# Two of eight depthwise convolutions computed by even and odd tokens on the matrix engine, and three smaller moves in a two-layer encoder trunk

## Chip, cores and metric

One core of a Trainium2 chip. The metric is the device time of one execution in microseconds (us). Its engines are named as in the profile: PE (TensorE, matrix products), PEld (its weight loads), DVE (VectorE), ACT (ScalarE), POOL (GpSimd) and SP (SyncE, which here issues nearly all DMAs).

## What is computed

A trunk of two layers on 512 tokens x 1024 features, float32. Each of four sub-layers is modulated by a vector c and closed by a gated residual and a LayerNorm:

```
def _modulation(c, w, b):
    m = jax.nn.silu(c) @ w + b
    shift, scale, gate = jnp.split(m, 3, axis=-1)
...
x <- LayerNorm(alpha*x + (1+gate) * f(x*(1+scale)+shift))
```

Layer 0 is a mixer (a spatial-gating MLP and a multi-scale pooling side by side), then a gated FFN with a depthwise convolution of width 3. Layer 1 is a conformer convolution, then a second FFN. The conformer convolution is

```
def _conformer_conv(h, w_in, dw, dw_b, ln_g, ln_b, w_out):
    a, g = jnp.split(h @ w_in, 2, axis=-1)
    z = a * jax.nn.sigmoid(g)
    z = _depthwise_conv(z, dw, dw_b)          # width 31, 1024 channels
    z = jax.nn.silu(_layer_norm(z, ln_g, ln_b))
    return z @ w_out
```

## The kernel before, in words

**Products.** Every large product runs on PE in three parts (`mm3`, L179): both operands are split into a high part that the fast fp32r format holds and a low remainder, and hi x hi, hi x lo and lo x hi are added in PSUM. `parts` (L150) splits a weight tile of 128x1024: ACT or DVE casts `whi`, DVE subtracts to `wlo`; both names have rings of 7 buffers. Activations are `hhi`/`hlo` or `ahi`/`alo` in the same way. A 512-column product has 512 columns of one operand streamed past 128x128 of the other.

**Opening (L124 to L520).** c is fetched into all 128 partitions (`cb`, 512 KB), ACT takes silu of it, and 24 PE transposes of a piece of `cb` against the identity (`WAKE`) follow. The modulation needs silu(c) @ w; DVE takes it as dots of rows of `in_ada` with `cb` (`ada_dot`, two per k, into the tiles `x`, which serve as staging). `project(k)` (L489) then scales the k-th block of x with them (ACT), splits it (`hhi`, `hlo`) and issues 24 products, 8 outputs of 3 parts each, output by output. k runs from 0 to 7. For k = 0 DVE makes both `whi` and `wlo`.

**FFN of layer 0 (about 145 to 511 us).** 22 pairs of 128 channels. Beside its PE work, `side0`/`ahead0` prepare layer 1: dots of the remaining modulations, split matrices of `cv_in` and `cv_out`, and 128x128 diagonal matrices, one per tap, that hold a tile's 128 tap weights (`diagonal`, L755, POOL, 2 x 62 steps). Split or built pairs are written to DRAM (`keep`) and later fetched into the `whi`/`wlo` rings (`recall`).

**Conv stage (about 511 to 700 us).** `to_next` (L397) closes the FFN: for each of four row tiles s of 128 tokens, DVE adds the residual, takes statistics, centres and scales `x`, PE transposes it, ACT modulates, DVE subtracts `hlo`. It then starts the first four column tiles of the next projection. The eight channel tiles follow: `proj_tiles` (two tiles `pa`, `pg`), `glu` (z = pa * sigmoid(pg), DVE), then the convolution of width 31 of that tile. The table `CONV` (L27) shares a tile's 31 taps out, for both halves of the tokens together or one by one: (number of taps on PE, number on POOL with ACT), the rest on DVE. A DVE tap is one SCALAR_TENSOR_TENSOR of 512 or 256 columns, a POOL tap an ACT scaling and a POOL addition, a PE tap three products of 256 columns with a diagonal matrix. Before, tile 6 has all 31 taps on PE in both halves, tile 7 has 31 on PE in the first half, tile 3 is wholly on DVE.

The two halves of the tokens (`hf`) are finished one after the other. `by_rows` (L936) transposes the convolved tiles `cvs` so that tokens are rows, and DVE takes statistics; the tiles come in the order of `CONV_END` (0, 2, 1, 3, 6, 4, 5, 7), two per call. `normalise` (L950) follows, `back` (L967) transposes again, applies gain, bias and silu (ACT) and splits, and `out` (L1017) adds the output product with the kept `cv_out` pairs. `advance(later[2], T_FILL)` places PE taps of the second half between `normalise` and `back`.

**The residual's affine step.** `finish_x` (L298) multiplies one half (d) of the columns of one row tile of x with the LayerNorm's gain row and adds its bias row: two steps. For the LayerNorm that stands before the conv stage these are 8 + 8 steps at the end of the stage: most of the first 8 on POOL, the last 8 on DVE (`finish(8, V, ...)`, L1042); the rows are fetched by `ln_rows` on ACT's queue at L986.

**Order.** Each engine runs its instructions in a fixed order. A scheduler writes it from the program order and its own estimates; `pin`, `behind` and the two flags `in_order`, `pool_order` hold pieces of it in the order of the program.

## Time and profile before

| what | value |
|---|---|
| median of 3 runs | 1071.51 us (1069.69 to 1071.95) |
| the profiled execution's own time | 1072.34 us |
| its span in the profile | 1070.6 us |
| mean granted clock of PE | 0.994 of full |
| DMA | 214.23 MB, mean 200 GB/s |

The span is the time from the first to the last instruction of the profiled execution; its own time has what lies around it too. Times in the rows below are us from the start of the span. A row of a timeline may stand for several equal instructions (x4), and its duration is then that of all. PE's products are pipelined: the distance from one start to the next is what a product costs, and the duration shown is longer. The profile puts nearly every instruction at L85, the helper that records them, so instructions are told apart by the names of their tiles.

### The profile page before, as it was taken

The page shows a single profiled execution, that of the slowest core. Times are in us where ns is not written, and L with a number is a line of the kernel's source. Part 1 is how long each engine was busy: PE and PEld are TensorE (multiplying, and loading weights), DVE is VectorE, ACT ScalarE, POOL GpSimd, SP SyncE. Part 2 cuts the span into 40 slices and gives each one's busy share as a digit, 9 for nine tenths or more (in the row PEclk, how much of TensorE's full clock was granted, in tenths as well). Part 3 has the DMA queues.
Part 4 walks back from the last instruction along what each step waited for, and adds up shares of the span by engine and source line. Part 5 has one row for each costly group of instructions (what it writes and reads, how often), then busy time and mean ns, then how long its engine had stood idle before and what let it go on. Part 6 is the DMA issues. An engine that isn't in the chain of part 4 may idle for free.

```text
span 1070.6 us, 13947 instructions
## 1 busy us (share of the span) xinstructions
PE 1046.3 (98%) x5157; PEld 883.5 (83%) x5157; DVE 787.3 (74%) x1173; ACT 461.4 (43%) x676; POOL 269.7 (25%) x309
## 2 busy tenths in 40 slices
PE   7999999999999999999999999899999999999997
PEld 5888798888888888888988987798888888888886
DVE  6789879989866889966399999767675333666537
ACT  4544374333743444533666743474444212444400
POOL 0000200068026950002199995200000022000011
PEclk9999999999999999999999999999999999999999
DMA  9969508777999998981555480233433233232302
GB/s 356 406 231 378 199 27 272 268 255 265 371 416 365 327 337 312 333 313 59 221 213 191 158 276 36 99 103 124 126 100 99 99 99 99 97 94 91 103 9 79
DMA packets 61555, 214.23 MB, mean 200 GB/s; under 512 B 6960, under 2 KB 6960, under 8 KB 61488
## 3 DMA queue, kind: packets, MB, share of 16 engines
q1 hardware_dynamic: 59184, 209.16, 54.7%
q10 hardware_dynamic: 2304, 4.20, 1.4%
q8 instruction: 40, 0.66, 0.2%
q14 instruction: 27, 0.22, 0.1%
HBM read 182.13 MB, written 31.20 MB: 199 GB/s over the span
## 4 chain that ended last, share of the span: by engine, by line
PE 87%; DVE 5%; DMA 3%; POOL 3%; issue 1%; ACT 0%; SPq 0%; DVEq 0%; POOLq 0%
PE ps L85 87%; POOL whi L85 1%; DVE a L85 1%; POOL wlo L85 1%; DMA w<-in_ffn_up 1%; DVE x L85 1%; DMA w<-in_ab_in 1%; DVE wlo L85 1%; DVE t L85 1%; DVE st L85 1%; DMA w<-in_cv_out 1%; DVE ps L85 1%; DMA whi<-keephi_cv_out 0%; ACT whi L85 0%; POOL x L85 0%
## 5 line engine op out<-in xcount | busy, mean ns | idle before, releaser
L85 PE MATMUL ps<-hhi,whi 128*128 128x512 f32 (+1 forms) x960 | 353.1, 369 | 0.0
L85 PE MATMUL ps<-hhi,wlo 128*128 128x512 f32 (+1 forms) x960 | 353.0, 368 | 0.1
L85 PE MATMUL ps<-hlo,whi 128*128 128x512 f32 (+1 forms) x960 | 353.0, 368 | 0.0
L85 DVE TENSOR_TENSOR wlo<-w,whi 128x1024 fp32r<-128x1024 f32 x176 | 218.3, 1246 | 164.8 <-ACT whi L85 160.9
L85 ACT CAST whi<-w 128x1024 fp32r<-128x1024 f32 x175 | 182.6, 1049 | 303.4 <-PE ps L85 185.7
L85 PEld LDWEIGHTS ps<-hhi,wlo 128*128 128x128 f32 x960 | 181.0, 189 | 30.5 <-DVE wlo L85 0.5
L85 PEld LDWEIGHTS ps<-hlo,whi 128*128 128x128 f32 x960 | 181.1, 189 | 29.8
L85 PEld LDWEIGHTS ps<-hhi,whi 128*128 128x128 f32 x960 | 180.7, 189 | 29.7
L85 POOL TENSOR_TENSOR x<-x,t 128x512 f32<-128x512 f32 x32 | 48.4, 1540 | 531.4 <-DVE t L85 531.4
L85 PE MATMUL ps<-whi,ahi 128*128 128x512 f32 (+1 forms) x426 | 165.4, 388 | 0.0
L85 PE MATMUL ps<-wlo,ahi 128*128 128x512 f32 (+1 forms) x426 | 164.3, 386 | 0.0
L85 PE MATMUL ps<-whi,alo 128*128 128x512 f32 (+1 forms) x426 | 164.2, 385 | 0.0
L85 DVE SCALAR_TENSOR_TENSOR t<-ps,cols,t 128x511 f32<-128x511 f32 x176 | 130.0, 744 | 5.9 <-ACT t L85 4.4
L85 POOL TENSOR_TENSOR a<-a 128x512 f32<-128x512 f32 (+1 forms) x99 | 104.5, 1092 | 22.9 <-ACT a L85 22.5
L85 ACT ACTIVATE t<-ps,cols 128x512 f32<-128x512 f32 (+1 forms) x108 | 78.0, 738 | 41.4 <-PE ps L85 39.7
L85 PEld LDWEIGHTS ps<-whi,ahi 128*128 128x128 f32 x426 | 80.1, 188 | 17.0 <-issue 0.5
L85 PEld LDWEIGHTS ps<-wlo,ahi 128*128 128x128 f32 x426 | 80.1, 188 | 16.4 <-issue 0.5
L85 PEld LDWEIGHTS ps<-whi,alo 128*128 128x128 f32 x426 | 80.1, 188 | 16.0
L85 ACT ACTIVATE a<-a,cols 128x512 f32<-128x512 f32 (+1 forms) x105 | 63.2, 634 | 27.0 <-POOL a L85 26.1
L85 DVE CUSTOM_DVE_ANT_0 w<-w,cb 128x1024 f32<-128x1024 f32 x56 | 69.7, 1254 | 6.3 <-DMA w<-in_ada 6.3
L85 DVE SCALAR_TENSOR_TENSOR ps<-a,cols,ps 128x512 f32<-128x512 f32 (+1 forms) x122 | 72.1, 660 | 0.0
L85 POOL TENSOR_SCALAR whi<-ident,taphi 128x128 fp32r<-128x128 f32 x62 | 46.8, 772 | 83.8 <-PE ps L85 77.3
(105 smaller groups left out, 988.7 us busy)
## 6 DMA issues: line engine op xcount, KB each, us to landing
w<-in_ffn_up SPq DMA_DIRECT2D x88, 512.0 KB, 4.1
w<-in_ada SPq DMA_DIRECT2D x56, 512.0 KB, 4.7
x<-in_ada SPq DMA_DIRECT2D x24, 512.0 KB, 7.4
w<-in_ffn_downA SPq DMA_DIRECT2D x24, 512.0 KB, 4.2
w<-in_ffn_downB SPq DMA_DIRECT2D x20, 512.0 KB, 4.4
w<-in_cv_in SPq DMA_DIRECT2D x16, 512.0 KB, 7.0
keephi_cv_in<-whi SPq DMA_DIRECT2D x12, 512.0 KB, 6.4
keeplo_cv_in<-wlo SPq DMA_DIRECT2D x12, 512.0 KB, 6.4
```

The source lines that it names most:

```text
L85: ins = getattr(self.engine, name)(*args, **kw)
```

## The change

1. *c as one row.* Two fetches of 2 KB bring c to one partition; ACT takes silu of the two rows; PE multiplies a column of ones with each (fp32, 128x512), and ACT and DVE copy the two results into `cb`. Six transposes of the identity stand before, 24 behind these products.
2. *First products kind by kind.* For k = 0 all eight hi x hi products go first, then the other two kinds, eight each.
3. *Two phase convolutions.* Tiles 3 and 6 (`PHASES`) go to PE wholly. Their z is written in two planes, even and odd tokens; four DMAs inside the chip put 64 channels x 2 phases on the 128 partitions; one matrix then holds two taps for each of two outputs, so a tile takes 2 halves x 16 pairs x 3 products of 256 columns. The result goes through an ACT copy, four DMAs (64x256) and an ACT step with the bias into `cvs`. They run after the projections of tiles 5 and 7. POOL builds their matrices with 16 steps of 128x1024. The other tiles share their taps anew.
4. *The affine step opens the stage.* Its rows are fetched in the FFN into two of the four buffers `w`; the halves d = 0 go to POOL, d = 1 to DVE, at the start of the conv stage.
5. DVE starts six taps of tile 0 at once (`V_FIRST`), `T_FILL` is 18, and `X_FILL`, `X_MID`, `X_LATE` are gone.

```diff
+PHASES = {3: 5, 6: 7}
 CONV = (
-    ((0, 12),), ((0, 31),), ((0, 0),), ((0, 0),), ((0, 17),), ((0, 17), (0, 20),), ((31, 0), (31, 0),), ((31, 0), (0, 8),),
+    ((0, 12),), ((0, 31),), ((0, 0),), (), ((0, 15),), ((0, 7), (0, 20),), (), ((0, 11), (18, 0)),
 )
...
-G_FILL, X_FILL, T_FILL = 6, 3, 21
-X_MID, X_LATE = 0, 1
+G_FILL, T_FILL = 6, 18
-WAKE = 24
+WAKE = 6, 24
...
-    fetch(cb, a["c"].partition_broadcast(P))
+    crow = [tmp()[0:1] for _ in range(2)]
+    for d in range(2):
+        fetch(crow[d], a["c"][:, d * 512 : (d + 1) * 512])
-    A.activation(cb, cb, AF.Silu)
...
+            for ps, l_, r_ in ops:
+                T.matmul(ps, l_[0], r_[0], start=True, stop=False)
+            for part in range(2):
+                for n, (ps, l_, r_) in enumerate(ops):
+                    h_low = part if n >= ST else 1 - part
+                    T.matmul(ps, l_[h_low], r_[1 - h_low], start=False, stop=False)
...
-        for _ in range(WAKE):
-            T.transpose(wake[:, 0:P], cb[:, 0:P], ident)
+        for _ in range(WAKE[0]):
+            T.transpose(wake[:, 0:P], ident, ident)
+        for d in range(2):
+            A.activation(crow[d], crow[d], AF.Silu)
+        for d in range(2):
+            ps = psum()
+            T.matmul(ps, ones[0:1], crow[d], start=True, stop=True)
+            (V.tensor_copy if d else A.copy)(cb[:, d * 512 : (d + 1) * 512], ps)
+        for _ in range(WAKE[1]):
+            T.transpose(wake[:, 0:P], ident, ident)
...
+    def phase_matrices(i, g):
...
+            G.tensor_tensor(
+                v.rearrange("p (j c) -> p j c", j=16),
+                mask.rearrange("p (o c) -> p o c", o=1).broadcast_to([P, 16, P // 2]),
+                one.broadcast_to([P, 16, P // 2]), ALU.mult,
+            )
+        keep(("phase", i, g), pair)
...
+        gbs = []
+        for n in ("lng_rows", "lnb_rows"):
+            w = xp.tile([P, 1024], F32, name="w", bufs=4)
+            Q.dma_start(w, a[n][1:2, :].partition_broadcast(P))
+            gbs.append(w)
...
+        def phase_operand(i, pa, sig):
...
+            two = z[:, 7 : 2 * PLANE + 9].rearrange("p (e i) -> p i e", e=2)[:, 0 : S // 2]
+            V.tensor_tensor(two, *(v.rearrange("p (i e) -> p i e", e=2) for v in (pa, sig)), ALU.mult)
...
+                    Q.dma_start(halves_[q * 64 : (q + 1) * 64, b], z[b * 64 : (b + 1) * 64, q * PLANE : q * PLANE + PLANE_LEN])
...
+            A.copy(zh, halves_)
+            V.tensor_tensor(zl, halves_, zh.bitcast(F32), ALU.subtract)
...
+        def phase_conv(i, z, groups):
+            ps = psum()
+            for b in range(2):
+                for m in range(PAIRS):
...
+                    mm3(ps[:, b * 256 : (b + 1) * 256], sl(groups[g], slice(None), at), sl(z, slice(None), b, slice(m, m + 256)), m == 0, m == PAIRS - 1)
+            y, yt = buf(), buf()
+            A.copy(y, ps)
...
+                    Q.dma_start(yt[b * 64 : (b + 1) * 64, odd * 256 : (odd + 1) * 256], y[odd * 64 : (odd + 1) * 64, b * 256 : (b + 1) * 256])
...
+            A.activation(*two, AF.Identity, bias=col("cv_dw_b", i))
...
+        for s in range(ST):
+            finish(s, 0, G)
+            finish(s, 1, V)
...
-        finish(X_LATE)
-        finish(8, V, last_v[0])
```

PE at the opening, before: `ident,cb` are the wake-up transposes.

```order
L85 MATMUL ps_118<-ident_84,cb_80 128x128 x24
L85 MATMUL ps_143<-whi_164,hhi_101 128x512
L85 MATMUL ps_143<-wlo_165,hhi_101 128x512
L85 MATMUL ps_143<-whi_164,hlo_102 128x512
L85 MATMUL ps_144<-whi_164,hhi_101 128x512
```

And now, up to the second k:

```order
L88 MATMUL ps<-ident 128x128 x6
L88 MATMUL ps<-t,ones 128x512 x2
L88 MATMUL ps<-ident 128x128 x24
L88 MATMUL ps<-whi,hhi 128x512 x4
L88 MATMUL ps<-hhi,whi 128x512 x4
L88 MATMUL ps<-whi,hlo 128x512 x4
L88 MATMUL ps<-hlo,whi 128x512 x4
L88 MATMUL ps<-wlo,hhi 128x512 x4
L88 MATMUL ps<-hhi,wlo 128x512 x4
```

The transposes no longer read `cb`, the two products that make it stand on PE ahead of 24 of them, and eight products that read only high parts come first.

DVE in `to_next` before the conv stage, from the second row tile to the third; x0 to x3 are the row tiles (the numbers behind are the program's), `st` the statistics, `mv` mean and variance. Before:

```order
L85 TENSOR_TENSOR x1_98<-x1_98,t_4417 128x512
L85 BN_STATS st_4247<-x1_98 128x6
L85 BN_AGGR mv_4421<-st_4247 128x2
L85 TENSOR_SCALAR rs_4423<-mv_4421 128x1
L85 TENSOR_SCALAR x1_98<-x1_98,mv_4421,rs_4423 128x512 x2
```

And now (`w_4208` and `w_4210` hold the gain and the bias):

```order
L88 TENSOR_TENSOR x1_100<-x1_100,t_4391 128x512
L88 TENSOR_TENSOR x0_99<-x0_99,w_4208 128x512
L88 BN_STATS st_4221<-x1_100 128x6
L88 TENSOR_TENSOR x0_99<-x0_99,w_4210 128x512
L88 BN_AGGR mv_4395<-st_4221 128x2
L88 TENSOR_SCALAR rs_4397<-mv_4395 128x1
L88 TENSOR_SCALAR x1_100<-x1_100,mv_4395,rs_4397 128x512 x2
```

Two affine steps of x0 stand between the residual add of x1 and its centring; the same holds for x1 in the rows of x2, and x2 in those of x3.

PE at the end of the second phase convolution, now. `a_4751` and `a_4753` are the convolved tiles 1 and 3, `a_4756`, `a_4754`, `a_4755`, `a_4757` the tiles 6, 4, 5 and 7; `a_5568` and `a_5569` are z of tile 7, high and low, and `whi_5695` its diagonal matrices.

```order
L88 MATMUL ps_5590<-a_5472,wlo_5556 128x256
L88 MATMUL ps_5720<-ident_86,a_4751 128x128
L88 MATMUL ps_5720<-ident_86,a_4753 128x128
L88 MATMUL ps_5724<-ident_86,a_4751 128x128
L88 MATMUL ps_5724<-ident_86,a_4753 128x128
L88 MATMUL ps_5765<-ident_86,a_4756 128x128
...
L88 MATMUL ps_5769<-ident_86,a_4757 128x128
L88 MATMUL ps_5792<-a_5568,whi_5695 128x256
L88 MATMUL ps_5792<-a_5569,whi_5695 128x256
L88 MATMUL ps_5792<-a_5568,wlo_5696 128x256
```

All 54 tap products of tile 7's second half now stand behind the eight transposes that need tile 6; before, the transposes of the first four tiles stood among the tap products, and 63 tap products stood between the last row transposes and the first `back`, 30 more behind that.

## Rows read from the trace of the kernel before

**Rows 1.** The profile page, part 1: busy time of each engine.

```profile
PE 1046.3 (98%) x5157; PEld 883.5 (83%) x5157; DVE 787.3 (74%) x1173; ACT 461.4 (43%) x676; POOL 269.7 (25%) x309
```

**Rows 2.** Waits of PE: releaser: us in total, times, longest.

```profile
PE ps L85 <- DMA whi<-keephi_cv_out: 3.1, 1, 3.1
PE ps L85 <- DVE a L85: 2.6, 3, 1.4
...
PE ps L85 <- DVE x L85: 0.8, 1, 0.8
```

**Rows 3.** Timeline, the opening: start us, us, engine, operation [idle before <-releaser].

```profile
0.74 0.38 SPq L85 DMA_DIRECT2D cb<-in_c  x1
...
5.29 1.06 ACT L85 ACTIVATE cb<-cb 128x1024 f32<-128x1024 f32 x1 [3.06 <-DMA cb<-in_c]
...
6.49 4.88 PE L85 MATMUL ps<-ident,cb 128*128 128x128 f32 x24 [6.49 <-ACT cb L85]
...
7.97 1.23 DVE L85 CUSTOM_DVE_ANT_0 x<-x,cb 128x1024 f32<-128x1024 f32 x1 [2.33 <-DMA x<-in_ada]
...
12.11 0.50 PE L85 MATMUL ps<-whi,hhi 128*128 128x512 f32 x1 [0.74 <-ACT hhi L85]
...
13.10 0.50 PE L85 MATMUL ps<-wlo,hhi 128*128 128x512 f32 x1 [0.48 <-DVE wlo L85]
```

**Rows 4.** Timeline of PE, first k of the input projection.

```profile
14.35 0.63 PE L85 MATMUL ps<-wlo,hhi 128*128 128x512 f32 x1
...
17.33 0.51 PE L85 MATMUL ps<-whi,hlo 128*128 128x512 f32 x1
17.68 0.39 PE L85 MATMUL ps<-hhi,whi 128*128 128x512 f32 x1
...
20.43 0.39 PE L85 MATMUL ps<-whi,hhi 128*128 128x512 f32 x1
```

**Rows 5.** Windows: us, busy of PE, PEld, DVE, ACT, POOL, clock, DMA share, GB/s.

```profile
10.80:14.10 3.30, 1.98 (x9) 1.06 (x8) 2.98 (x4) 2.27 (x3) 0.00 (x0) 1.00 1.03 410
14.20:17.50 3.30, 3.30 (x9) 2.51 (x9) 3.24 (x7) 1.07 (x2) 0.00 (x0) 0.50 1.02 405
676.40:679.70 3.30, 3.30 (x9) 2.51 (x9) 1.75 (x3) 0.00 (x0) 0.00 (x0) 0.50 0.00 0
```

**Rows 6.** Groups of instructions, whole span: fp32 products, copies from PSUM.

```profile
L85 ACT COPY gate<-ps 128x512 f32<-128x512 f32 x8 | 4.4, 586 | 1.0 <-PE ps L85 1.0
...
L85 PE MATMUL ps<-t,pw 128*128 128x512 f32 x8 | 3.8, 592 | 0.0
```

**Rows 7.** DMA issues, at 604 to 640 and from 1050 on: KB each, us to landing.

```profile
wlo<-keeplo_cv_out SPq DMA_DIRECT2D x6, 512.0 KB, 6.3
...
out_y<-x SPq DMA_DIRECT2D x6, 256.0 KB, 2.0
```

**Rows 8.** Windows of the FFN of layer 0, columns as in rows 5.

```profile
410.00:450.00 40.00, 39.90 (x176) 32.77 (x175) 37.02 (x55) 20.12 (x26) 0.00 (x0) 1.00 0.89 299
```

**Rows 9.** Timelines of DVE and PE, opening of the conv stage.

```profile
509.18 1.00 DVE L85 TENSOR_SCALAR x<-x,mv,rs 128x512 f32<-128x512 f32 x2 [0.66 <-POOL rs L85]
...
510.38 1.04 PE L85 MATMUL ps<-ident,x 128*128 128x128 f32 x8
```

**Rows 10.** Timeline of PE, first half of the convolution to the first output product.

```profile
624.37 0.60 PE L85 MATMUL ps<-ident,a 128*128 128x128 f32 x4
...
626.19 0.48 PE L85 MATMUL ps<-a,whi 128*128 128x256 f32 x2
...
633.63 0.28 PE L85 MATMUL ps<-a,wlo 128*128 128x256 f32 x1
...
640.59 0.48 PE L85 MATMUL ps<-whi,a 128*128 128x512 f32 x1
```

**Rows 11.** Timeline of DVE in the conv stage.

```profile
635.71 2.04 DVE L85 SCALAR_TENSOR_TENSOR ps<-a,cols,ps 128x256 f32<-128x256 f32 x5
...
651.95 3.09 DVE L85 TENSOR_TENSOR x<-x,a 128x512 f32<-128x512 f32 x5
```

More of the change, by code (lines that the diff above doesn't have):

```diff
@@ L762, in diagonal @@
         keep(("diag", i, g), pair, n * P)
+    def phase_matrices(i, g):
+        at = sorted(PHASES).index(i) * 4 * PAIRS + 16 * g
+        pair = tuple(wp.tile([P, 1024], F32R, name=name, bufs=7) for name in ("whi", "wlo"))
+        for v, t in zip(pair, (ph_hi, ph_lo)):
+            one = t[:, at : at + 16].bitcast(F32).rearrange("p (j o) -> p j o", o=1)
+            G.tensor_tensor(
[4 more added lines that the diff above has]
+        keep(("phase", i, g), pair)
     def ahead0():
@@ L776, in side0 @@
             V.tensor_tensor(taps_lo, taps, taps_hi.bitcast(F32), ALU.subtract)
-        if i >= 9 and todo_d:
-            diagonal(*todo_d.pop(0))
+            raw = tmp(len(PHASES) * 4 * PAIRS)
+            Q.dma_start(raw, a["phase_taps"])
+            A.copy(ph_hi, raw)
+            V.tensor_tensor(ph_lo, raw, ph_hi.bitcast(F32), ALU.subtract)
+            V.tensor_tensor(mask, ident[:, 0 : P // 2], ident[:, P // 2 :], ALU.add)
+        if i >= 9:
+            if todo_p:
+                phase_matrices(*todo_p.pop(0))
+            elif todo_d:
+                diagonal(*todo_d.pop(0))
         if i in (13, 15, 17):
@@ L879, in glu @@
                 behind(A.activation(warm, mhalf, AF.Silu), sigmoid)
+            if i in PHASES:
+                phased[i] = phase_operand(i, pa, sig), []
+                return
             z = buf(S + 2 * HALO)
@@ L921, in body @@
                     gate = gate_bcast(gate_column(2))
+                for t_, after in PHASES.items():
+                    if after == i:
+                        phase_groups(t_, phased[t_][1], 4)
                 if i + 1 < KD:
@@ L927, in body @@
                 advance(now[1], G_TAPS)
+            else:
+                advance(now[0], V_FIRST)
+            for t_, after in PHASES.items():
+                if after == i:
+                    phase_conv(t_, *phased[t_])
+                    if i + 1 < KD:
+                        advance(now[0], V_TAPS)
+                        advance(now[1], G_TAPS)
             advance(todo_d, D_TAPS)
@@ L984, in back @@
                 behind(A.activation(warm, mhalf, AF.Gelu_apprx_tanh), soft)
-        gbs = [ln_rows(1, d, buf) for d in range(2)]
         while any(now):
@@ L995, in body @@
                 by_rows(0, (0, 1), 4)
-        rest = [(s, d) for d in range(2) for s in range(ST)]
-        def finish(n, eng=G, after=None):
-            for _ in range(min(n, len(rest))):
-                s, d = rest.pop(0)
-                finish_x(s, d, gbs[d], eng, after)
         advance(later[1], G_FILL)
-        finish(X_FILL)
         join(0, CONV_END)
@@ L1095, in _bands, with _phases @@
     return out
+def _phases(dw):
+    import numpy as np
+    taps = np.zeros((2, P // 2, len(PHASES), 2, PAIRS, 2), np.float32)
+    for n, i in enumerate(sorted(PHASES)):
+        for half in range(2):
+            f = slice(i * P + half * P // 2, i * P + (half + 1) * P // 2)
+            for q in range(2):
+                for m in range(PAIRS):
+                    for odd in range(2):
+                        j = 2 * m + 1 - q - odd
+                        if 0 <= j < TAPS:
+                            taps[q, :, n, half, m, odd] = dw[j, f]
+    return taps.reshape(P, -1)
 def _pack(i):
@@ L1144, in _pack @@
     o["band"] = _bands()
+    o["phase_taps"] = c(_phases(i["cv_dw"][0]))
     parts = {
```

45 lines of the change are left out of this document (37 added, 8 removed).

## Prediction

> **What bounds the kernel now.** I read the busy times first: TensorE (PE) works 98% of the span, so nothing else can be worth much unless it shortens PE's own work, its idle time or its half-speed time [rows 1]. Then PE's waits: they are few, and two of those that this change touches lie in one stage, the conformer convolution (511 to 700 us): 2.6 us in three waits for the split halves `a` from DVE, and 3.1 us in one wait for the 8th pair of kept `cv_out` matrices [rows 2]. Third, the opening, in order of time: c's 512 KB are issued at 0.74 and have landed at 5.29, ScalarE (ACT) turns them into silu(c) in one 1.06 us step, PE's 24 wake-up transposes need that, VectorE (DVE) starts its dots with it at 7.97, and PE's first product starts at 12.11 [rows 3]. Fourth, the spacing of products: .23 us each from 17.68 to 20.43 (12 steps), but .43 us each from 14.35 to 17.33 (7 steps) [rows 4]; the windows show why, the granted clock there is at the lower of its two levels (1.2 against 2.4 GHz) [rows 5]. Something within 0.2%, about 2.1 us, can't be told from no change by a measurement of this kernel.
>
> **The sum** is made against the profiled execution's own 1072.34 us; the median of the runs shown, 1071.51, is 0.83 less, and I take that off at the end.
>
> *Opening: c as one row, products by kind.* Removed: the 512 KB landing before silu, and 24 transposes that wait for it. Added before the dots: a 2-KB landing, silu of two rows, two fp32 products ones x row, two copies. A 2-KB landing is not in the trace; I bound it by 2.0 us, the quickest landing that I found [rows 7], and 4.5 us, that of the 512 KB it replaces [rows 3], and take 3, nearer to the quick one as nothing stands in front of it. Two such products cost 3.8 / 4 = .95 us each [rows 6] with PE at full clock, up to twice that at half. So: issue .7, landing to 3.8, silu to 5.0, products to 7.2, copy of 512 columns from PSUM .59 [rows 6]: cb stands near 7.9 (7.5 to 8.8). The dots started at 7.97, when their own matrix had landed [rows 3]; with 512 KB less in front it lands no later. So the first product stays near 11.9 (11.7 to 12.8): cb's new road costs nothing as long as it hides behind that landing. The gain is in what follows. Before, the second product waited for `wlo` and came at 13.10 [rows 3]; now eight products that need only `whi` and `hhi` come first, and PE is not idle in the two us before the stretch that was at half speed. If the clock then stays at the upper level, 24 products x .229 = 5.5 us bring the second k at 17.4 instead of 20.43: **-3.0 us** (bounds -3.4 and -0.3). PE has no idle time after that until a wait of 0.8 us for DVE `x`, at the end of this stage, the only one of its kind [rows 2]; what DVE does there starts from PE's own last products, so the gain is carried past it.
>
> *FFN of layer 0: matrices.* 88 of the 124 POOL steps that build one 128x128 matrix each go, 16 that build eight or more at once come, and 11 groups are kept instead of 8, some 2 MB more written. POOL is busy beside PE; nothing on PE waits for it. The DMA engines are busy .89 of the time at 410 to 450, where PE still loses only 0.1 us [rows 8]. I take **0** (bounds -0.3, if that 0.1 and its like vanish, to +4, if cover is gone and one 512 KB load is late by its landing time).
>
> *Residual's affine steps at the opening of the conv stage.* Eight go to POOL, eight to DVE. On DVE they stand inside the chain that centres x for the transposes: x of the row tile before is multiplied and added between the residual add and the statistics of the next. A step is 3.09 / 5 = .62 us [rows 11]; two of them fill gaps of dependent steps, so I take 1.1 per row tile rather than 1.24. Before, the third tile's centring began at 509.18 and its transposes ran at 510.38, with no gap [rows 9], so PE was just served. Now its centring is 2 x 1.1 = 2.2 late, of which the earlier slack of about 0.9 is taken off: **+1.3** (0.7 to 2.2). The last tile has slack enough, since 48 products stand ahead of it.
>
> *First half of the convolution.* PE's tap products of 256 columns: before 186 ahead of the transposes at 624.37, then 63 and 30 more; now 192 in two phase convolutions, and 54. One costs (633.63 - 626.19) / 62 = .12 us [rows 10]. In all 33 fewer, -4.0; but the first 192 are 6 more than 186, so they end at 624.4 + 0.7 + 1.3 = 626.4. Then the order is the matter: PE's next rows are 4 transposes of finished tiles (to 626.9) and 8 that need tile 6, whose result takes an ACT copy from PSUM (.59) [rows 6], four transfers whose issues take SP some .38 each [rows 3], a landing of 2.0 or more [rows 7], and an ACT step of .6. That is 631.1 at the earliest; a landing like `wlo` of cv_out, 6.3 in that stretch [rows 7], gives 635.4. I take 632.4, nearer to the quick end, as 64 KB move and not 512: PE idle 5.5 us. Before, 63 taps filled this time (626.19 to 633.63); now all 54 stand behind the transposes. Transposes to 633.4, fillers to 639.9, and from the row transposes to the second normalised tile it took 635.71 - 626.19 = 9.5 before [rows 10, 11]; with fewer taps between, 8: 641.4. Then back-transposes; DVE has seven taps of .4 [rows 11] ahead of the first cast, so the first output product comes near 645.1, against 640.59 [rows 10]: +4.5, of which 1.3 is told above: **+3.2** (0 to +6.5).
>
> *Second half.* The eight DVE steps (5 us from 651.95 on) are gone [rows 11], so most of the 2.6 us of waits for `a` goes; I leave 0.7: **-1.9** (-2.6 to 0). The wait for the 8th cv_out pair stays, as its first buffer comes free no sooner: 0.
>
> *Clock.* Before, soon after that wait of 3.1 us [rows 2], PE ran at half from 676.4 to 679.7 [rows 5], a loss of 1.7 us. With the shorter waits ahead this may go (half a chance, -0.8); the new idle time at 627 to 632 may bring the same, against which the fillers have a spare us (+0.5). **-0.3.**
>
> Sum: -3.0 + 0 + 1.3 + 3.2 - 1.9 - 0.3 = -0.7, or 1071.6 for the profiled execution and 1070.8 for the median. With the uncertainty of the large terms, the forecast's own range is 1068.8 to 1072.8: no change that can be told.
>
> **The rivals.** *A: the round trip is hidden.* If tile 6's values return by 631.1 and DVE, relieved of 26 taps and 8 steps, keeps its casts early, the +3.2 is gone and so is the second half-speed time: -0.7 - 3.2 - 0.5 = -4.4, or 1067.1. For it: DVE is busy without a gap in that stage and is relieved. Against it: the order, with every filler behind the transposes.
>
> *B: tile 6 returns late (slower).* The four transfers stand on SP's queue behind the first four cv_out pairs; the last two of these loads start when PE frees their buffers, just before. If each of tile 6's transfers takes the 6.3 us of such a load, not 3.3, PE idles 8.5 us instead of 5.5, and the sum is -0.7 + 3.0, with 0.8 more for a half-speed stretch, or 1074.6. It decides from an idle time of about 7.5 us on. Against it: the loads of this stretch were not dense, and 256 KB landed in 2.0 [rows 7]. The Trainium skill (DMA: Bandwidth & Descriptors, Queues, rings and completion order) says that descriptors of one engine are taken in ring order, and that a semaphore lands only after all earlier writes of that engine; by that rule the wait of this rival would come whenever a load is under way on the same engines. No run so far shows a small transfer behind a large one.
>
> *C: the opening stays at half speed.* If transposes of the identity don't raise the clock, the products start at half and rise 4.3 us later, as PE before was at full by 10.8, having started at 6.49 [rows 3, 5]: 10 products x .43, 14 x .2275, second k at 19.4: gain 1.0 instead of 3.0, or 1072.8. Against it: before, PE had done nothing but transposes until 12.11 [rows 3], and the granted clock from 10.8 to 14.1 was 1.00 [rows 5]. The Trainium skill (TensorE: Matmul & The Clock Gate, on the transpose mode) says that the full clock doesn't engage for transposes, since they don't count as PE being busy; by that rule C holds, and the trace of this kernel speaks against it.
>
> *D: the opening doesn't do what it says*, because cb is later than the dots' matrix; each us over 7.97 takes one us from the 3.0. This is in the range of the first term.
>
> **How the numbers follow.** Forecast .40, A .27, B .22, C .11. Faster than 1069.4: A, and a quarter of the forecast's range, .37. Slower than 1073.7: B, .22. The rest, .41, is within. The range, 1065.5 to 1075.5, takes in A with its clock term and B with some of the layer-0 bound.
>
> **What would show it.** Second k at 17.4 with clock 1.00 from 12 to 18; PE waiting about 1.3 us at its third transposes near 510; an idle stretch of some 5 us right behind the second phase convolution, ended by ACT or a transfer of tile 6; first output product about 5 us later than before; the waits for `a` near 666 gone. Wrong, if PE doesn't stop behind that convolution (A), if the first products are .43 apart (C), or if the 390 to 450 stretch of the FFN has idle PE.

## The result, and the profile after

The changed kernel takes 1088.74 us (median of 4 runs, 1086.53 to 1091.03) against 1071.73 for the kernel before (4 runs). The ratio of the runs is 1.0155, with a 95% interval of 1.0121 to 1.0190: slower by 16.6 us, outside the range of the prediction (1065.5 to 1075.5). The profiled execution took 1086.53 us with a span of 1084.7, 14.1 us more than before. PE's busy time, from the page's part 1:

```profile
PE 1050.4 (97%) x5134; PEld 883.5 (81%) x5134; DVE 804.2 (74%) x1169; ACT 459.5 (42%) x673; POOL 241.4 (22%) x230
```

PE has 23 instructions fewer than in [rows 1] and is busy 4.1 us longer; the other 10.0 us of the 14.1 are idle time. DVE takes 16.9 us more for four instructions fewer: in the mean they got longer. This is a first sign of the main cause. Waits of PE after (releaser: us in total, times, longest):

```profile
PE ps L88 <- ACT a L88: 7.4, 1, 7.4
PE ps L88 <- ACT whi L88: 5.6, 2, 3.2
PE ps L88 <- DVE x L88: 4.0, 5, 1.2
PE ps L88 <- DMA whi<-keephi_cv_out: 3.0, 1, 3.0
PE ps L88 <- DVE hlo L88: 1.9, 1, 1.9
PE ps L88 <- DVE a L88: 1.7, 3, 0.8
```

Against [rows 2], the wait for the 8th cv_out pair stands as it was, the waits for `a` from DVE went from 2.6 to 1.7, and three kinds are new or grown: one for tile 6's values (ACT a), two for split weights in the FFN (ACT whi), and those at the opening of the conv stage (DVE x and hlo). Where they lie, on the timeline of PE after (start us, us, engine, operation [idle before <- releaser]):

```profile
11.78 1.20 PE L88 MATMUL ps<-whi,hhi 128*128 128x512 f32 x4 [0.47 <-ACT hhi L88]
...
17.56 0.50 PE L88 MATMUL ps<-whi,hhi 128*128 128x512 f32 x1
...
387.79 0.50 PE L88 MATMUL ps<-hhi,whi 128*128 128x512 f32 x1 [3.25 <-ACT whi L88]
...
414.65 0.50 PE L88 MATMUL ps<-hhi,whi 128*128 128x512 f32 x1 [2.32 <-ACT whi L88]
...
508.33 1.12 PE L88 MATMUL ps<-ident,x 128*128 128x128 f32 x8 [1.22 <-DVE x L88]
...
519.74 1.11 PE L88 MATMUL ps<-ident,x 128*128 128x128 f32 x8 [1.10 <-DVE x L88]
...
536.87 0.39 PE L88 MATMUL ps<-hlo,whi 128*128 128x256 f32 x1 [1.94 <-DVE hlo L88]
...
646.12 2.33 PE L88 MATMUL ps<-ident,a 128*128 128x128 f32 x8 [7.43 <-ACT a L88]
...
658.65 0.50 PE L88 MATMUL ps<-whi,a 128*128 128x512 f32 x1 [0.81 <-DVE a L88]
...
691.01 0.50 PE L88 MATMUL ps<-whi,a 128*128 128x512 f32 x1 [2.99 <-DMA whi<-keephi_cv_out]
```

At the waits of 3.25, 2.32 and 7.43 us PE falls to the lower clock, and in the opening it no longer does, as the windows show (us, busy of PE, PEld, DVE, ACT, POOL, clock, DMA share, GB/s):

```profile
14.00:17.50 3.50, 3.50 (x16) 2.58 (x14) 3.08 (x7) 1.43 (x3) 0.00 (x0) 1.00 1.03 410
389.20:392.60 3.40, 3.40 (x9) 2.64 (x10) 3.40 (x5) 0.94 (x2) 2.82 (x3) 0.51 0.67 181
416.50:419.90 3.40, 3.40 (x10) 2.63 (x9) 3.40 (x5) 0.61 (x1) 0.00 (x0) 0.51 0.80 181
641.80:652.00 10.20, 5.78 (x26) 5.24 (x27) 5.16 (x17) 1.12 (x2) 0.53 (x1) 0.50 0.16 52
```

The first two of the lower stretches lie behind their waits. The third begins 4.3 us before its wait ends (646.12), so that products run at half speed for 5.9 us, from 646.12 to 652.0.

So the account of stages, from PE's timeline in each profiled execution. "Gate columns" is the start of the eight transposes `ident,gcol`, some 120 us into the FFN of layer 0; "FFN" is the time from there to the conv stage's first transposes of x, without the wait just before these; "opening wait" is that wait; "conv" runs from those transposes to the product that the 8th cv_out pair releases. The experiments are in the same table, with the ratio of their runs to the kernel before.

| kernel | gate columns | FFN | opening wait | conv | span | ratio (95%) |
|---|---|---|---|---|---|---|
| before | 266.52 | 233.84 | 0 | 174.58 | 1070.6 | 1 |
| after | 263.77 | 243.34 | 1.22 | 182.68 | 1084.7 | 1.0155 (1.0121 to 1.0190) |
| e1, opening alone | 263.16 | 235.01 | 0 | 174.21 | 1069.2 | .9997 (.9980 to 1.0013) |
| e3, rows in other tiles | 263.18 | 241.19 | 0 | 178.73 | 1078.2 | 1.0074 (1.0052 to 1.0097) |
| e13, POOL's affine steps later | 263.17 | 242.9 | .27 | 180.68 | 1080.7 | 1.0122 (1.0091 to 1.0153) |
| e9, e3 with short POOL steps | 263.17 | 237.29 | 0 | 179.63 | 1074.2 | 1.0046 (1.0027 to 1.0066) |
| e12, e3 without phases | 263.15 | 235.7 | 0 | 170.89 | 1065.4 | .9964 (.9948 to .9981) |

From before to after: -2.75 until the gate columns, +9.5 in the FFN from there, +1.22 at its end, +8.1 in the conv stage, and -1.7 behind it (the half-speed stretch at 676 of [rows 5] is gone, and the rest is the same work): +14.4 at PE's last instruction, of which the span shows 14.1. Each row is one execution, and parts of the program that are the same in two kernels differ in them by up to half a microsecond or more (the gate columns stand at 263.15 to 263.84 in the kernels with the same opening).

### The profile page after: what moved, and what is told of

It is laid out like the page before. It is cut to its first block, busy times and chain, and to the rows that moved or that the text cites. A ratio compares the mean times of both kernels' runs of the same rounds, so it can differ in the third digit from the quotient of the medians.

```text
span 1084.7 us, 13879 instructions
## 1 busy us (share of the span) xinstructions
PE 1050.4 (97%) x5134; PEld 883.5 (81%) x5134; DVE 804.2 (74%) x1169; ACT 459.5 (42%) x673; POOL 241.4 (22%) x230
## 4 chain that ended last, share of the span: by engine, by line
PE 81%; DVE 7%; DMA 7%; ACT 2%; issue 2%; POOL 1%; SPq 1%; DVEq 0%; ACTq 0%; POOLq 0%
PE ps L88 81%; DVE wlo L88 2%; DMA w<-in_ffn_up 2%; DMA w<-in_ffn_downB 2%; DVE x L88 2%; ACT whi L88 1%; DMA w<-in_cv_out 1%; DMA x<-in_ada 1%; DVE t L88 1%; DVE ps L88 1%; POOL whi L88 1%; SPq L88 1%; DVE st L88 1%; POOL x L88 0%; DMA a<-a 0%
## 5 line engine op out<-in xcount | busy, mean ns | idle before, releaser
L88 DVE TENSOR_TENSOR wlo<-w,whi 128x1024 fp32r<-128x1024 f32 x176 | 226.0, 1292 | 163.5 <-ACT whi L88 160.0
L88 POOL TENSOR_TENSOR x<-x,t 128x512 f32<-128x512 f32 x32 | 52.3, 1662 | 539.3 <-DVE t L88 475.8
L88 POOL TENSOR_TENSOR a<-a 128x512 f32<-128x512 f32 (+1 forms) x90 | 95.8, 1101 | 19.8 <-ACT a L88 19.3
L88 ACT ACTIVATE a<-a,cols 128x512 f32<-128x512 f32 (+1 forms) x98 | 58.8, 642 | 35.0 <-POOL a L88 24.0
L88 ACT CAST ahi<-t 128x512 fp32r<-128x512 f32 x52 | 32.2, 619 | 86.9 <-DVE t L88 86.8
L88 DVE SCALAR_TENSOR_TENSOR ps<-a,cols,ps 128x512 f32<-128x512 f32 (+1 forms) x113 | 61.3, 615 | 0.0
```

The lines of the kernel that those rows point to most:

```text
L88: ins = getattr(self.engine, name)(*args, **kw)
```

## Experiments

The theories were these. For the FFN: POOL's long steps hold up DVE (port), or the rows that sit in two of the four buffers `w`, or the 2 MB more of traffic, make weight loads late (loads). For the opening of the conv stage: DVE's own eight added steps, or POOL's eight beside them. For the conv stage: the round trip of tile 6's values, or merely the order of PE's work around it.

**The mechanism, read from the trace first.** The 16 POOL steps that build a phase matrix are long; groups of POOL by shape (xcount | busy us, mean ns | idle before):

```profile
L88 POOL TENSOR_TENSOR whi<-mask,phhi 128x1024 fp32r<-128x1024 f32 x8 | 21.0, 2627 | 103.2 <-PE ps L88 96.4 <-DMA keephi_cv_in<-whi 6.8
...
L88 POOL TENSOR_TENSOR wlo<-mask,phlo 128x1024 fp32r<-128x1024 f32 x8 | 20.0, 2506 | 0.0
```

POOL beside two of them, and beside the residual's steps (timeline of POOL, after):

```profile
373.52 2.06 POOL L88 TENSOR_TENSOR whi<-mask,phhi 128x1024 fp32r<-128x1024 f32 x1 [10.12 <-PE ps L88]
375.54 2.88 POOL L88 TENSOR_TENSOR wlo<-mask,phlo 128x1024 fp32r<-128x1024 f32 x1
...
525.37 12.59 POOL L88 TENSOR_TENSOR x<-x,w 128x512 f32<-128x512 f32 x8
```

And DVE in the same microseconds (timeline of DVE, after):

```profile
371.99 1.22 DVE L88 TENSOR_TENSOR wlo<-w,whi 128x1024 fp32r<-128x1024 f32 x1
...
375.17 4.33 DVE L88 TENSOR_TENSOR wlo<-w,whi 128x1024 fp32r<-128x1024 f32 x2
...
525.44 2.91 DVE L88 TENSOR_SCALAR x<-x,mv,rs 128x512 f32<-128x512 f32 x2 [0.66 <-POOL rs L88]
528.27 3.46 DVE L88 TENSOR_TENSOR hlo<-t,hhi 128x512 fp32r<-128x512 f32 x2
531.66 3.48 DVE L88 TENSOR_TENSOR x<-x,w 128x512 f32<-128x512 f32 x2
```

One `wlo` takes 1.22 us when POOL is idle; two that meet the phase steps take 4.33 instead of 2.4. Beside POOL's affine steps every pair of DVE steps takes 2.9 to 3.5 us; [rows 9] has the first of these pairs at 1.00. In the FFN the delay goes on through SP's fixed order: the late `wlo` ends at 379.50, its write to DRAM is issued then, and two loads of `ffn_up` behind it. Timeline of SP, after, and the row of these loads in the DMA view of 378 to 390 (xcount, KB each, us to landing):

```profile
379.53 0.32 SPq L88 DMA_DIRECT2D keeplo_cv_out<-wlo  x1
379.90 1.63 SPq L88 DMA_DIRECT2D w<-in_ffn_up  x2
```

```profile
w<-in_ffn_up SPq DMA_DIRECT2D x2, 512.0 KB, 7.0
```

So they land near 387. ACT casts the first at 386.69, and PE has waited 3.25 us when it goes on at 387.79. (For the cast the profile names POOL's diagonals, which stand behind the two phase steps and end at 386.2; they and the landing lie too close together to be told apart.) The Trainium skill (SBUF — State Buffer, Who interferes with whom) has this rule: a DVE instruction with two SBUF inputs contends with a GpSimd instruction that reads SBUF, and the one that issues second is blocked until the other ends. The rows of `wlo`, `hlo` and x<-x,w above agree with it, and the DVE steps that read one operand from PSUM are as long as ever (744 ns in the mean at 310 to 430, before and after). The pair at 525.44 has one wide operand and two columns; this sentence of the rule does not cover it, and it grew as well.

**e1: the opening alone** (the kernel before with parts 1 and 2).

```diff
-    fetch(cb, a["c"].partition_broadcast(P))
+    for d in range(2):
+        fetch(crow[d], a["c"][:, d * 512 : (d + 1) * 512])
...
+            for ps, l_, r_ in ops:
+                T.matmul(ps, l_[0], r_[0], start=True, stop=False)
```

> The kernel before with the opening of the change alone (c as one row; first products kind by kind). Theory: the opening does what it was meant to do, second k near 17.4 us with the clock at 1.00, and the 3 us are carried to the end: about 3 us faster than the kernel before, 1068 to 1069.5. Rival: the gain seen in the changed kernel's opening is given back at the end of the first stage (wait for x near 133 us): within 1 us of the kernel before.

Measured: 1071.31 against 1071.81, ratio .9997 (.9980 to 1.0013). The gain is there, 3.36 us at the gate columns, but 1.2 of it is given back inside the FFN, at a place where PE before was just served (timeline of PE, e1):

```profile
407.01 0.50 PE L85 MATMUL ps<-hhi,whi 128*128 128x512 f32 x1 [0.60 <-ACT whi L85]
...
408.27 0.50 PE L85 MATMUL ps<-hhi,wlo 128*128 128x512 f32 x1 [0.53 <-DVE wlo L85]
```

Another 1.2 goes behind the 8th cv_out pair, where PE is at half speed for 6.8 us and not 3.4. What is left at the end, 1.4 us of span, is less than the interval. The opening is no part of the loss.

**e2: the affine step back at its late places** (after, without part 4).

```diff
-        for s in range(ST):
-            finish(s, 0, G)
-            finish(s, 1, V)
...
+        finish(3)
...
+        finish(1)
+        finish(8, V, last_v[0])
```

> The changed kernel with the residual's affine steps and their rows back at the end of the conv stage. Theory: these steps and the two w buffers cost 5.4 us of PE waits at 508 to 537 us (five waits); without them these waits go, and about 2 us of waits for a come back near the end of the stage: 3 to 5 us faster than the changed kernel, about 1084 to 1086. Rival: the waits at 508 to 537 come from the late FFN loads, which have nothing to do with the rows: they stay, and the time is that of the changed kernel, 1088.

Measured: 1091.24, ratio 1.0181 (1.0151 to 1.0212), no faster than after, where 3 to 5 us were expected: a miss. PE's waits from 508 to 537 are gone as expected, but the conv stage takes 189.4 us instead of 182.7, with new waits for DVE (a: 2.75, 1.48 and .88; t: 1.33 and 1.11) and 20.5 us at the lower clock instead of 10.2. With phases in the kernel, DVE has no room for these steps at the end. That is read from the waits of this one kernel and was not tried further.

**e3: the rows of gain and bias in other tiles** (`cb`, which is no longer needed, and the `gate` tile), so that all four buffers `w` serve the loads.

```diff
-            w = xp.tile([P, 1024], F32, name="w", bufs=4)
-            Q.dma_start(w, a[n][1:2, :].partition_broadcast(P))
+        gbs = [None, row_pair(cb, 1)]
...
+        gbs[0] = row_pair(xp.tile([P, D], F32, name="gate", bufs=1), 0)
```

> The changed kernel with the affine steps where they are, but their rows in tiles that are free then (the broadcast c and the gate), so that the ring w has four buffers for the last nine loads of the stage. Theory ring: two held buffers of four starve those loads and push their splits into DVE's chain; PE's waits at 508 to 537 fall from 5.4 us to about 1.3, the time by about 4 us, to 1084 to 1085. Rival chain: the affine steps in DVE's chain are what costs; the waits stay within 1 us of 5.4, the time near 1088.

Measured: 1079.96, ratio 1.0074, half of the loss. In the FFN 2.15 us come back, but not because the buffers shorten PE's waits there. DVE's `wlo` are as long as in after (1566 ns against 1568 at 310 to 430). The waits are 1.90 + 1.54 and 2.32 + .52 us, 6.3 in all against 6.7 after, and e13 below, whose rows sit in `w` as in after, has the same 6.3 (2.06 + 1.37 and 2.32 + .53). The other 1.75 us are the half-speed stretch of 416.5: after and e13 have it, e3 has none behind the same wait, and has one of 3.4 us behind the 8th cv_out pair instead. Why it moved is open. So nothing here shows that the held buffers cost time in the FFN up to 415.

At its end they do cost something: with all four buffers the last `wlo` of the stage starts at 497.49, with two at 503.35 (501.35 in e13), and the opening wait is 0 against 1.22 (.27 in e13). In the conv stage another 4.0 us come back: of the waits at its opening only the 1.10 for DVE's own steps is left. But e3 does two things there: since `gate` comes free late, POOL's steps also start later (its first waits 2.55 us for the row). e13 was made to tell them apart.

**e13: only POOL's affine steps later** (after, with one POOL step ahead of them that needs the last `hlo`).

```diff
+        held = sm.tile([P, 1], F32, name="held")
+        G.tensor_tensor(held, h[1][:, KD - 1, S - 1 : S].bitcast(F32), mhalf, ALU.mult)
         for s in range(ST):
```

> The changed kernel (rows in two of four w buffers) with one POOL step of 128x1 ahead of POOL's eight affine steps that reads the last element of hlo, so that they start when DVE has made the last low half, 538 us, and not at 525. Theory port: in the changed kernel DVE's steps at 525 to 538 take 13.3 us instead of 5.0, beside POOL's; apart from them they take 5 us, and the last three of PE's five waits (0.39, 0.75, 1.94 us) go, the first two (1.22 and 1.10) stay: 3 to 4 us faster than the changed kernel, 1084 to 1086. Theory ring: e3 gained by its free w buffers alone; all five waits stay, the time is the changed kernel's, 1088.

Measured: ratio 1.0122 (1.0091 to 1.0153), span 1080.7, 4.0 less than after. The same DVE steps as above, before POOL's affine steps begin at 530 (timeline of DVE, e13):

```profile
523.44 1.00 DVE L88 TENSOR_SCALAR x<-x,mv,rs 128x512 f32<-128x512 f32 x2 [0.66 <-POOL rs L88]
524.36 1.29 DVE L88 TENSOR_TENSOR hlo<-t,hhi 128x512 fp32r<-128x512 f32 x2
525.56 1.41 DVE L88 TENSOR_TENSOR x<-x,w 128x512 f32<-128x512 f32 x2
```

2.91, 3.46 and 3.48 have become 1.00, 1.29 and 1.41, and the waits of .39, .75 and 1.94 us behind them are gone; the 1.10 stays. That shows POOL's steps beside DVE's as the cause of these three waits. They are worth less than their 3.1 us: the conv stage is 2.0 us shorter, since the waits for `a` further on grow from 1.7 to 2.9. The other 2 us of the 4.0 lie ahead of POOL's steps (.6 before the gate columns, .4 in the FFN, .95 at its end), where the edit changes nothing, and the intervals of the two ratios overlap: the reading rests on the rows, not on the time. The other 2 us that e3 gains in the conv stage are not explained by it and were not traced further.

**e4: the 18 taps ahead of tile 6's transposes** (after).

```diff
+        advance(later[2], T_FILL)
         by_rows(0, (2, 3))
...
-        advance(later[2], T_FILL)
```

> The changed kernel with the 54 tap products of tile 7 ahead of the transposes that need tile 6. Theory: they cover the return of tile 6; PE's wait of 7.4 us falls to about 1, the half-speed stretch of 10 us goes, and the first output product comes 5 to 8 us earlier: 1081 to 1084. Rival: the chain behind the transposes (statistics, normalising, DVE's casts) sets the first output product; the idle time moves behind the transposes and the time falls by under 2 us.

Measured: 1088.67, ratio 1.0151: no difference from after. PE's wait for tile 6 falls from 7.43 to 2.87 us, but the taps are then missing behind the transposes, where PE waits 5.21 and .90 us for DVE's `t`. The idle time moves: in either order of PE's fillers the chain from tile 6 through ACT, DMA, PE and DVE sets the time.

**e5: the diagonals first, then the phase matrices** (after), **and e6: e3 and e5 together.**

```diff
-            if todo_p:
-                phase_matrices(*todo_p.pop(0))
-            elif todo_d:
+            if todo_d:
                 diagonal(*todo_d.pop(0))
+            elif todo_p:
+                phase_matrices(*todo_p.pop(0))
```

> The changed kernel with the three groups of diagonal matrices (POOL, 16 steps, 13 us each) built before the eight groups of phase matrices (2 steps, 5 us each) and not after them. Theory: the long builds hold buffers of the whi ring late in the FFN, where pairs of cv_out are split too, and ACT's next split waits for them; built first they are covered: PE's 6.7 us of waits for whi and wlo at 387 to 416 and the half-speed stretches behind them go, 1079 to 1081. Rival: 11 groups and their 2 MB more are too many at either order; the waits move but stay above 4 us, 1086 to 1089.

> Both repairs: rows of the affine step in free tiles and diagonal matrices first. If both act by themselves the gains add: 1088.7 - 8.8 - 8.5, about 1071 to 1072, the kernel before's time, with the wait for tile 6 (7.8 us) still there. If the diagonals' waits have another cause: about 1080.

Measured: e5 1089.15, ratio 1.0166 (1.0135 to 1.0197); e6 1086.50, 1.0142. Neither helps: the FFN takes 246.4 and 246.8 us, more than after. The long steps have moved to another place and do the same there. POOL in e5:

```profile
402.45 2.88 POOL L88 TENSOR_TENSOR wlo<-mask,phlo 128x1024 fp32r<-128x1024 f32 x1
...
408.69 2.08 POOL L88 TENSOR_TENSOR whi<-mask,phhi 128x1024 fp32r<-128x1024 f32 x1 [3.36 <-DMA keephi_cv_out<-whi]
```

and DVE in e5:

```profile
403.49 2.92 DVE L88 CUSTOM_DVE_ANT_0 w<-w,cb 128x1024 f32<-128x1024 f32 x1
...
407.78 1.22 DVE L88 CUSTOM_DVE_ANT_0 w<-w,cb 128x1024 f32<-128x1024 f32 x1
...
408.93 2.39 DVE L88 TENSOR_TENSOR t<-t 128x512 f32<-128x512 f32 x1
```

The dot at 403.49, which met a POOL step, took 2.92 us, and the next, which met none, 1.22; the step on `t`, .69 us elsewhere, took 2.39 beside the next POOL step.

**e7: the four return transfers on ACT's queue** (e6).

```diff
-                    Q.dma_start(yt[b * 64 : (b + 1) * 64, odd * 256 : (odd + 1) * 256], y[...])
+                    A.dma_start(yt[b * 64 : (b + 1) * 64, odd * 256 : (odd + 1) * 256], y[...])
```

> As e6, with the four transfers of each phase convolution's result issued by ACT and not by SP. Theory queue: they stand behind a cv_out pair on SP's queue and rings; on ACT's they land in 2 to 3 us instead of 4.6 to 5.9, and PE's wait falls from 7.8 to 4 to 5.5 us: 3 us faster than e6. Rival load: the DMA engines are shared and loaded with cv_out, the landing stays at 4.5 us or more and PE's wait above 6.5: within 1 us of e6.

Measured: 1085.19, ratio 1.0130 (1.0099 to 1.0162) against e6's 1.0142 (1.0118 to 1.0165): not told apart. The transfers land in 4.4 us instead of 5.6, and PE waits 6.72 instead of 8.09 us. SP's queue is a small part of the trip.

**e8: no return trip** (e6; the phases' results are not put back into the order of the tokens, and the copy and the four transfers are left out).

```diff
-            A.copy(y, ps)
-            for b in range(2):
-                for odd in range(2):
-                    Q.dma_start(yt[...], y[...])
-            A.activation(*two, AF.Identity, bias=col("cv_dw_b", i))
+            A.activation(cvs[i], ps, AF.Identity, bias=col("cv_dw_b", i))
```

> As e6, with the return of the two phase convolutions left out: ACT writes the result with the bias straight into its tile, in the wrong order of channels and tokens. It prices the trip. Theory: PE's wait of 7.8 us goes but for about 1, and so does the half-speed stretch of 10 us behind it: 8 to 12 us faster than e6. Rival: DVE's chain (statistics, normalising, casts) is next in line and takes half of it back: 3 to 6 us faster than e6.

Measured: 1078.45, ratio 1.0066 (1.0044 to 1.0087); the conv stage takes 171.6 us against e6's 180.8. So the trip costs the stage 9.2 us in these executions (8.1 of time by the two ratios); PE's wait falls by 7.6 of them, from e6's 8.09. Timeline of PE in e8, with what is left of that wait in the first row:

```profile
635.42 0.87 PE L88 MATMUL ps<-ident,a 128*128 128x128 f32 x6 [0.45 <-ACT a L88]
...
647.15 0.50 PE L88 MATMUL ps<-whi,a 128*128 128x512 f32 x1 [1.08 <-DVE a L88]
...
680.42 0.50 PE L88 MATMUL ps<-whi,a 128*128 128x512 f32 x1 [2.69 <-DMA whi<-keephi_cv_out]
```

**e9: e3 with the phase matrices built in pieces of 128 columns**, eight POOL steps for one.

```diff
-            G.tensor_tensor(
-                v.rearrange("p (j c) -> p j c", j=16),
+            for c in range(0, 16, 2):
+                G.tensor_tensor(
+                    v.rearrange("p (j c) -> p j c", j=16)[:, c : c + 2],
```

> As e3 (rows elsewhere), with each POOL step of 128x1024 that builds phase matrices cut into 8 steps of 128x128, in the old order of groups. Theory: a POOL step of 2 to 3 us holds up DVE's steps between two SBUF operands for its whole length (a dot of 1.22 us took 2.92 beside one); DVE's lost time delays the splits of ffn_up, and PE waits 6.3 us at 386 to 415. Short steps let DVE in between: the mean of wlo at 310 to 430 falls from 1.57 to about 1.35 us, PE's waits to 2 us or less: 1072 to 1075. Rival count: 11 groups kept, not 8, and their DMA are the cause; waits stay above 4.5 us, 1078 to 1081. Rival sum: POOL's total time counts and not the length of a step; DVE's means stay, the waits too.

Measured: 1077.30, ratio 1.0046 (1.0027 to 1.0066). The FFN falls by 3.9 us to 237.3, the stall near 387 is gone, and DVE's `wlo` group at 310 to 430 is back near that of before. DVE's groups by shape in that window (xcount | busy us, mean ns | idle before), before and after:

```profile
L85 DVE TENSOR_TENSOR wlo<-w,whi 128x1024 fp32r<-128x1024 f32 x28 | 36.3, 1304 | 15.3 <-ACT whi L85 15.1
L88 DVE TENSOR_TENSOR wlo<-w,whi 128x1024 fp32r<-128x1024 f32 x24 | 37.3, 1568 | 10.4 <-ACT whi L88 10.3
```

then e9:

```profile
L88 DVE TENSOR_TENSOR wlo<-w,whi 128x1024 fp32r<-128x1024 f32 x25 | 33.3, 1340 | 13.9 <-ACT whi L88 13.8
```

The same matrices are built from the same operands on the same engine; only the length of one step differs. What hurts is how long POOL holds on, not how much it does: in e9 POOL is busy with them for longer altogether (3.81 to 5.94 us for eight pieces in its timeline at 361 to 388, against a mean of 2.5 to 2.6 for one step; 94 us in all against 41). The intervals of e3 and e9 overlap, so it is the stall, the FFN and DVE's mean that carry this, not the time alone.

**e10: 48 transposes of the identity ahead of tile 6's** (e9), to hold the clock up.

```diff
+        for n in range(48):
+            pin(T.transpose(rows[1, n % 2][:, 0:P], ident, ident))
         by_rows(0, (2, 3))
```

> As e9, with 48 transposes of the identity on PE between the second phase convolution and the transposes that wait for tile 6; their result is overwritten. They take about 6.2 us of the 7.8 us wait and cost nothing by themselves. Theory clock: the 10 us at half speed behind that wait are an effect of the idle time; they go or shrink below 4 us, and the time falls by 2 to 5 us against e9. Rival: that stretch is bound by DVE's chain anyway (its waits for a), and the clock there is worth under 1 us; or transposes don't keep the clock up, and the stretch stays.

Measured: 1078.05, ratio 1.0061 (1.0042 to 1.0079): no gain. PE still waits 3.34 us after the 48, as tile 6 came later than in e9 (its four transfers land in 6.1 us, not 4.6; why is not shown). The time at the lower clock falls from 10.2 to 6.8 us, but mostly inside the wait: right behind it PE runs at half speed for 3.4 us, against 4.0 in e9. So this run does not price the clock. What sets the time there is seen on DVE: from its first statistics of tile 6 to its first cast it works without a gap, 10.9 us in e9, in e10 and in after (646.85 to 657.79).

**e11: two taps of tile 7 fewer on PE, so 10 kept groups instead of 11** (e9).

```diff
-    ... (), ((0, 11), (18, 0)),
+    ... (), ((0, 11), (16, 0)),
```

> As e9, with 16 and not 18 taps of tile 7's second half on PE (DVE takes two more), so that two groups of diagonals are kept, 10 groups in all. Theory count: what is left of PE's waits in the FFN of layer 0 (2.8 us at 408) comes from the last group, built and written when cv_out is split too; it falls below 1 us and the stretch from the gate columns (263 us) to the transposes near 500 from 237.3 to 235.5: about 2 us faster than e9. Rival: the wait comes from loads that are late there in every version (0.3 us in the kernel before, 1.1 in e1); it stays at 2 to 3 us, within 1 us of e9.

Measured: 1076.69, ratio 1.0048 (1.0033 to 1.0063), as e9. PE's waits of .73 and 2.76 us at 397 to 411 stay. So one group fewer does not take them away. They lie where e1 has .60 + .53 and e12 1.40 + .53, a place near 408 where PE before was just served. In e12 the cast waits .95 us there for its load of `ffn_up`; in after and e9 it stands, in ACT's order, behind a gelu that waits for PE's own sums. Why the stall is 1 to 2 us longer with phases stays open.

**e12: the opening and the affine step, no phases** (the kernel before with parts 1, 2 and 4, the rows as in e3).

```diff
+        for s in range(ST):
+            finish_x(s, 0, gbs[0], G)
+            finish_x(s, 1, gbs[1], V)
...
-        finish(X_LATE)
-        finish(8, V, last_v[0])
```

> The kernel before with the opening of the change and the affine steps at the opening of the conv stage (rows in free tiles), without phase convolutions. Theory: the steps cost about 1.1 us of PE's time at their new place (as in e3) and give back the 2.3 us of waits for a at 650 to 668, the opening 1.5 to 3 us: 1068 to 1070, faster than the kernel before by 2 to 4 us. Rival: DVE is late there for its taps, not for these steps; the waits stay and the time is that of e1, 1071 to 1072.

Measured: 1066.87 (11 runs) against 1071.09 (19 runs), ratio .9964 (.9948 to .9981): the fastest kernel of this study, by 4.2 us faster than before. Timeline of PE in e12; the rows answer to [rows 9] and to the waits of [rows 2]:

```profile
510.21 1.11 PE L85 MATMUL ps<-ident,x 128*128 128x128 f32 x8 [1.05 <-DVE x L85]
...
662.03 0.50 PE L85 MATMUL ps<-whi,a 128*128 128x512 f32 x1 [0.28 <-DVE a L85]
...
669.77 0.51 PE L85 MATMUL ps<-whi,a 128*128 128x512 f32 x1 [2.77 <-DMA whi<-keephi_cv_out]
```

The affine step costs 1.05 us at its new place and takes away nearly all of the 2.6 us of waits for `a`, and the 1.6 us that PE before waited for `t` are gone too; the conv stage is 3.7 us shorter than before.

**The loss in shares of the time before**, each from two ratios, with an interval worked out from theirs: what e3 undoes (the rows in `w` and POOL's steps at once beside DVE's), 1.0155 - 1.0074 = .81% (.40 to 1.22; 8.7 us); the long steps of the phase matrices, 1.0074 - 1.0046 = .28% (-.02 to .58; 3.0 us), by itself not clear of noise; the rest of the phases, 1.0046 - .9964 = .82% (.56 to 1.08; 8.8 us); the other parts, a gain of .36% (.19 to .52; 3.9 us). By stages the 8.8 are 8.7 in the conv stage, about the 9.2 of e8's trip, 1.6 in the FFN and 1.5 less behind the conv stage.

## Why the prediction was wrong, by its steps

*Opening, -3.0: right in size.* `cb` stood at 7.51 us (7.9 forecast), the first product came at 11.78 (11.9), the second k at 17.56 (17.4), with the clock at 1.00 from 14.0 to 17.5. Rival C is refuted by this: between 6.71 and 11.3 PE had done nothing but transposes of the identity, and it ran at the upper level behind them. The rise can be seen in their spacing, .21 us up to 10.4 and .11 from there. The Trainium skill (TensorE: Matmul & The Clock Gate, Part 4: PE-mode transpose) states the opposite; here the measurement decides. Rival D is refuted as well. The gain was carried past the wait for x, as forecast (.55 us at 131, .84 before); that it is not whole at the end was not foreseen: e1 loses 1.2 us of it at 407 and 1.2 behind the conv stage.

*FFN of layer 0, 0 (-0.3 to +4): wrong, +9.5, and the largest miss.* The sentence that failed is "POOL is busy beside PE; nothing on PE waits for it". The stalls of 3.25 + .58 and 2.32 + .53 us and two half-speed stretches of 3.4 us, which lose about half their length, make 10 us. The second stall is idle PE at 390 to 450, a sign of being wrong that the prediction had named. The first stall, with its stretch, is due to the length of POOL's steps: in e9 it is gone, and the FFN is 3.9 us shorter than in e3. The second stands near 408 without long steps (e9), with one group fewer (e11) and, at 1.40 + .53 us and without a half-speed stretch, without phases (e12); what makes it longer with phases stays open, and the held buffers are not shown to (e3, e13). I compared the number of POOL steps and never asked which engine shares something with POOL: the step was costed by what waits for its result, not by what it runs beside.

*Affine steps at the opening, +1.3 (0.7 to 2.2): right for DVE, incomplete for POOL.* PE waits 1.10 us at its third transposes, and e13 and e12 (1.05) show that this is DVE's own steps. But 1.22 us stand ahead of the first transposes and .39 + .75 + 1.94 behind the third: 5.4 in all. The 1.22, 18 us ahead of POOL's steps, go with the late splits at the end of the FFN (e3). For the other three I gave DVE's eight steps a price and POOL's eight none; these run for 12.59 us just when DVE makes x and `hlo`, and hold it up (e13).

*First half, +3.2 (0 to +6.5): right in mechanism, too small.* From the first transposes to the first output product it took 150.3 us against 140.2 before; without the 4.2 us of the waits just told, that is +5.9. The trip, first on ACT's timeline of after:

```profile
638.29 0.58 ACT L88 COPY a<-ps 128x512 f32<-128x512 f32 x1 [2.60 <-PE ps L88]
...
645.32 0.75 ACT L88 ACTIVATE a<-a,cols 128x512 f32<-128x512 f32 x1 [3.14 <-DMA a<-a]
```

then on SP's, and in the DMA view of 634 to 648 (xcount, KB each, us to landing):

```profile
639.04 2.38 SPq L88 DMA_DIRECT2D a<-a  x4
```

```profile
a<-a SPq DMA_DIRECT2D x4, 64.0 KB, 5.4
```

An issue takes 2.38 / 4 = .59 us, not .38, and a landing 5.4, not 3.3; so the wait is 7.43 us, not 5.5: that is 1.9 of the 2.7 by which the term was too small. Another .9 is that the phase convolutions end 1.6 us later than the 186 products of before, the told waits aside, and not .7. Behind the wait the path was as forecast, 12.5 us from the transposes to the first output product against 12.7: PE's 5.9 us at half speed, against "a spare us (+0.5)", did not lengthen it, as DVE sets it. Rival B has the mechanism, a late tile 6, with a wait between forecast and rival.

*Second half, -1.9: right.* From the first output product to the 8th cv_out pair it took 32.36 us against 34.35, -2.0, and that pair's wait stayed. *Clock, -0.3:* the stretch at 676 did go; the new one, at 642 to 652, cost little where it stands, and the two that cost time lie in the FFN, where none was forecast. Rival A is refuted by the wait of 7.43 us, and the other order of the fillers (e4) does not hide the trip either. Its "26 taps" also left something out: DVE has 26 steps of 512 columns fewer on its taps (57 for 83), but 17 of 256 columns more (56 for 39).

## What to carry to other kernels

Cost a step on POOL by its length and by the DVE steps beside it that read two SBUF operands, not only by who waits for its result; where such work must stay on POOL, cut it into short steps or start it when DVE reads PSUM (not tried here). Moving data between partitions by DMA in the middle of a chain costs its whole length (copy, issues, landing, step), here 9.2 us of a stage; compare that sum with the products saved before anything else. When parts of a change are independent, run them apart: here the opening and the affine step with its rows in free tiles gave 0.36%, and the phases, with the rows in `w`, took 1.9%.

## What was not expected of the hardware

- DVE and POOL: a POOL step of 2 to 2.9 us makes a DVE step of 1.22 us with two SBUF operands last up to 2.92, and POOL's 128x512 affine steps make pairs of DVE steps of 1.0 to 1.4 us last 2.9 to 3.5. The POOL steps lose less: the eight affine steps take 12.59 us, and 10.51 in e13, where DVE has little to do beside them.
- Transposes against the identity brought PE to the upper clock. In the kernel before nothing else ran: 24 from 6.49 on, .21 us apart until 10.8 and .11 behind. After it was the same at 10.4, with no other product before 11.78 than four instructions that multiply one row, and the clock was 1.00 from 14.0 to 17.5 us.
- With waits of 3.25 + .58 and 2.32 + .53 us, two products between the two waits of each pair, PE ran at .51 of its full clock for 3.4 us behind them; e3, with 2.32 + .52 at the second place, kept the upper clock there. In the wait of 7.43 us the clock fell at 641.8, and it was .50 up to 652.0.
